# A triangular solve in two 8x8 blocks instead of one of 16x16, and an output norm whose channel scale and bias go into its other products

## The chip, the core and the metric

One core of a Trainium2 chip runs the kernel. Its engines are TensorE (PE, matrix products, with the loading of weights listed apart as PEld), VectorE (DVE), ScalarE (ACT), GpSimd (POOL) and SyncE (SP, which issues DMAs). Each has its own queue of instructions, worked off in order; they meet in SBUF and in PSUM, and wait for each other by semaphores. The metric is the device time of one execution in microseconds, the median of several runs.

## The reference, cut to what matters

One sequence of 256 tokens of width 1024 goes through two layers. Each layer is a feed-forward block, a mixer with three branches (a recurrent one with 8 heads of 64, a global attention and a window attention, each gated), and a second feed-forward block. The change is in the recurrent branch:

```python
def step(state, inp):                       # one token, one head; forwards and backwards over the sequence
    r_t, w_t, k_t, v_t, a_t, b_t = inp
    sa = jnp.einsum('bhij,bhj->bhi', state, a_t)
    state = (state * w_t[:, :, None, :] + sa[..., None] * b_t[:, :, None, :]
             + v_t[..., None] * k_t[:, :, None, :])
    return state, jnp.einsum('bhij,bhj->bhi', state, r_t)
...
mean = jnp.mean(wkv, axis=-1, keepdims=True)
var = jnp.mean(jnp.square(wkv - mean), axis=-1, keepdims=True)
y = ((wkv - mean) * lax.rsqrt(var + LNX_EPS)).reshape(bsz, s, RWKV_DIM) * lnx_g + lnx_b
y = y + bonus.reshape(bsz, s, RWKV_DIM)
gate = jax.nn.sigmoid(gl) @ g2
return y * gate
```

The sum over tokens is worked out in chunks of 64 tokens; within a chunk it needs the inverse of a unit lower triangular 64x64 matrix for each head and direction. Everything is float32.

## The kernel before, in words

Each matrix product of weights with activations is split: weights and activations are each a high part (`w_hi`, made by ACT or DVE at L62 or L64) and a rest (`w_lo`, made by DVE or GpSimd at L93), and three products are summed in PSUM (L52 is the line of every matmul, L55 that of every transpose on PE). Weights stream from HBM all the time. The feed-forward blocks are untouched by the change.

`Mixer.run` makes the mixer's work out of Python generators, one for each kind of work: Q (projections of the attentions), R (projections of the recurrent branch), A and V (attention scores and values), K (the normalised keys, `kk_norm`), P (`prep`, decay and learning rates), O (`post`, the output norm), F (`branches`: the gates `gt` and the output projections `wo`), and 0 to 3, the four units of the recurrence. Unit u has the head half `hf` = u//2 and the direction `d` = u%2. The string `ORDER` names, letter by letter, which generator goes on to its next `yield`. The strings in `ENG` name, for each kind of helper, the engine of each call in turn: a is ACT, v DVE, p GpSimd. A list scheduler of the framework then orders the instructions of each engine from this program, so the order of the rows on an engine isn't that of the letters alone.

In unit `wkv(u)`, `Lp` are products of 64x64 blocks, masked into `LL`; `T` are transposes, copied to `LL` and `Z`. When d is 1, the 16x16 diagonal blocks of both directions are copied into `sol` (`blocks()`, picks `K`), transposed so that each of them lies in one lane (L839), and solved by substitution on DVE (L842 to L851): for s from 1 to 14 a multiply (L847) and an add (L848). The result goes back by transposes (L852, L857: `Tn`). This happens once for each half: the first solve (unit 1) and the second solve (unit 3) of a layer, four in the program. From 16x16 to 32x32 one step of refinement on PE follows, `gp` (32 small matmuls a unit), a subtraction on DVE (L864) and `tp` (32 more), then L871 and the transposes L872; then the same from 32 to 64. The first `gp` and `tp` are worked off for both units d = 0 and 1 together.

`post()` takes the two halves in turn: the mean by a product with `bones`, the variance by `head_rsqrt` (products `hs`, DVE at L693, a power on GpSimd at L694, ACT at L696, products `hb` with the head's identity, which spread 1/rms over PSUM), then L985 (y times 1/rms), L988 (channel scale and bias), `bonp` (the bonus sum) and `gatep`, L995 (bonus times v), L996 (add) and L997 (times the gate). All of it is on DVE.

Of the kernel before, what the change touches and what calls it, by code (L numbers as in the profile page):

```python
# [11 lines left out]
ALU = mybir.AluOpType  # L12
AX = mybir.AxisListType
# [322 lines left out]
ORDER = 'QQQQQQRRQQRQKRRRQQARARAQARAKARRRKPVVAAARFARARVVPPAAAAAVFPVAAAAFFFVFVFFPFF00FF1F10F01011F1F010F01100F00001P12010F0F211111PF2OFFFPF23F233F3FO3F3223O2232F2332323323223F323OOOFFFFF'  # L336
ENG = {'Q': 'pvvxxxvwvvvv', 'R': 'xxwvxxvwvvvvvvv', 'F': 'wpxxxvppvpppxxpppwpvvwxxwpvvppppwxxp', 'M': 'vvvppvvv', 'O': 'vvvvvvvv', 'T': 'vavaaavvaaavavaa', 'G': 'vvavav', 'K': 'avaaaaavavaaaaaa', 'C': 'aavaavavvaavaavaaaaavaav', 'U': 'aavvavvaaaavavav', 'Y': 'avavvaavaaaaaavvavvaaaav', 'H': 'vvvv', 'J': 'vaavvaaa'}
KAP = float(np.exp(-0.5))
R_MU, R_W0, R_A0, R_KK, R_KA, R_RK, R_LG, R_LB, R_N = 0, 15, 23, 31, 35, 39, 43, 47, 51
# [16 lines left out]
class Mixer:  # L356
# [426 lines left out]
    def wkv(self, u):  # L783
        nc, n = self.nc, self.n
        V, mm = nc.vector, n.mm
        hf, d = u // 2, u % 2
# [3 lines left out]
        x = (v if d == 0 else v[:, :, ::-1]).rearrange("p a (c t) -> p a c t", c=4)  # L790
# [5 lines left out]
        if d == 1:  # L796
            scr = self.scr = self.t([128, 1024], "sol", tag="bk", bufs=2)
# [39 lines left out]
        if d == 1:  # L837
# [3 lines left out]
            Dm = Df.rearrange("p (t s) -> p t s", t=16)  # L841
            V.scalar_tensor_tensor(Dm, sol[:, :, 0:16], n.lane[:, 0:1], sol[:, :, 16:32], ALU.mult, ALU.add)  # L842
            stmp = scr[:, 768:832]
            for s in range(1, 15):
                m = 15 - s
                tv = stmp[:, :m * s].rearrange("p (t c) -> p t c", t=m)
                V.tensor_tensor(tv, Dm[:, s + 1:16, s:s + 1].to_broadcast([128, m, s]), Dm[:, s:s + 1, 0:s].to_broadcast([128, m, s]), ALU.mult)  # L847
                V.tensor_tensor(Dm[:, s + 1:16, 0:s], Dm[:, s + 1:16, 0:s], tv, ALU.add)  # L848
            V.memset(Df[:, 0:256:17], 1.0)
            V.tensor_scalar(sol[:, :, 0:16], Dm, n.lane[:, 0:1], None, ALU.mult)  # L850
# [3 lines left out]
        scr = self.scr  # L854
# [108 lines left out]
    def post(self):  # L963
        nc, n = self.nc, self.n
        V, mm = nc.vector, n.mm
        for hf in range(2):
# [18 lines left out]
            V.tensor_tensor(y, y, rb, ALU.mult)  # L985
            for pp in range(2):
                p = 2 * hf + pp
                self.pick("O").tensor_scalar(y[:, pp, :], y[:, pp, :], self.par[:, R_LG + p:R_LG + p + 1], self.par[:, R_LB + p:R_LB + p + 1], ALU.mult, ALU.add)  # L988
# [7 lines left out]
            self.pick("O").tensor_tensor(y, y, bon, ALU.add)  # L996
# [134 lines left out]
```

## Time and profile before

| | us |
|---|---|
| median of three runs | 1452.02 (1450.62 to 1454.06) |
| the profiled execution | 1456.31 |
| its span (first to last instruction) | 1454.4 |
| PE busy in the span | 1401.1 |
| DVE, ACT, POOL busy | 1004.6, 744.4, 206.2 |

The profile is of one execution, 4.3 us above the median. The span is 1.9 us shorter than that execution's time; the rest lies before the first and behind the last instruction. A row of the time line tells when instructions of one line started, how long they took, and in brackets how long the engine had been idle before and what it waited for. [...] "issue" is idle time for which the profile shows no cause.

### The profile page before, as it was taken

To read this page: it belongs to the slowest core of one execution; us is meant where nothing else is said; L and a number is where in the kernel's file an instruction comes from. 1 tells how busy PE (TensorE), PEld (TensorE's weight loads), DVE (VectorE), ACT (ScalarE), POOL (GpSimd) and SP (SyncE) were. 2 spreads that over 40 slices of the span, in tenths; PEclk is the share of its full clock that TensorE was granted. 3 is DMA by queue.
4 is the path that set the end of the run, shared out by engine and by line. 5 is a ranking of instruction groups with operands and counts; after the bars stand their busy time and mean duration, and the time that the engine had idled before them with its cause. 6 is when DMAs were issued, how large, how long until landed. Compare 5 with 4: busy or idle time off the path is not lost.

```text
span 1454.4 us, 25957 instructions
## 1 busy us (share of the span) xinstructions
PE 1401.1 (96%) x10482; PEld 1158.6 (80%) x10482; DVE 1004.6 (69%) x1518; ACT 744.4 (51%) x1241; POOL 206.2 (14%) x181
## 2 busy tenths in 40 slices
PE   7999999999998999999999999999998989999997
PEld 6888878877786878888888888788676868788886
DVE  5677467886867576776467864789758766668753
ACT  6555334665444355555455553356553443655543
POOL 0000033104315100000000000522041241000001
PEclk9999999999999999999999999999999999999999
DMA  7766656423314047666566666563243131576663
GB/s 219 209 201 187 195 152 190 130 70 120 113 50 144 27 144 205 189 191 194 162 188 196 190 192 191 159 182 100 67 132 102 49 114 48 167 207 188 189 191 112
DMA packets 113436, 220.24 MB, mean 151 GB/s; under 512 B 7362, under 2 KB 32164, under 8 KB 113316
## 3 DMA queue, kind: packets, MB, share of 16 engines
q1 hardware_dynamic: 111328, 215.08, 49.4%
q10 hardware_dynamic: 1508, 2.58, 0.5%
q8 instruction: 82, 1.34, 0.4%
q0 software_dynamic: 480, 0.93, 0.3%
q14 instruction: 38, 0.31, 0.1%
HBM read 217.51 MB, written 1.05 MB: 150 GB/s over the span
## 4 chain that ended last, share of the span: by engine, by line
PE 74%; DVE 8%; issue 8%; ACT 4%; DMA 3%; POOL 3%; SPq 0%; POOLq 0%; ACTq 0%; DVEq 0%
PE dn L52 19%; PE gt L52 18%; PE up L52 17%; PE gu L52 3%; PE wo L52 3%; PE rk L52 3%; DVE w_lo L93 2%; DMA w_raw<-in_w_in 2%; PE yp L52 1%; POOL w_lo L93 1%; PE Lp L52 1%; PE tp L55 1%; PE sc L52 1%; ACT w_hi L62 1%; DMA w_raw<-in_ffn_w_up 1%
## 5 line engine op out<-in xcount | busy, mean ns | idle before, releaser
L93 DVE TENSOR_TENSOR w_lo<-w_raw,w_hi 128x1024 fp32r<-128x1024 f32 (+1 forms) x360 | 444.1, 1234 | 252.0 <-ACT w_hi L62 248.5
L62 ACT ACTIVATE w_hi<-w_raw 128x1024 fp32r<-128x1024 f32 x358 | 379.8, 1062 | 403.4 <-PE dn L52 118.6
L52 PE MATMUL dn<-w_hi,aT 128*128 128x512 f32 x704 | 218.2, 390 | 0.0
L52 PE MATMUL gt<-hT,w_hi 128*128 128x512 f32 x512 | 179.0, 395 | 0.0
L52 PE MATMUL up<-hT,w_hi 128*128 128x512 f32 x512 | 178.2, 394 | 0.0
L52 PEld LDWEIGHTS dn<-w_hi,aT 128*128 128x128 f32 x704 | 131.9, 188 | 27.9 <-DVE sg L268 0.9
L93 POOL TENSOR_TENSOR w_lo<-w_raw,w_hi 128x1024 fp32r<-128x1024 f32 x50 | 123.5, 2474 | 149.4 <-ACT w_hi L62 91.1
L52 PE MATMUL gt<-hT,w_lo 128*128 128x256 f32 x512 | 142.2, 278 | 0.0
L52 PE MATMUL up<-hT,w_lo 128*128 128x256 f32 x512 | 141.8, 277 | 0.0
L52 PE MATMUL gt<-w_hi,hT 128*128 128x512 f32 x384 | 138.3, 421 | 0.0
L52 PE MATMUL dn<-w_lo,aT 128*128 128x512 f32 x352 | 137.7, 391 | 0.0
L52 PEld LDWEIGHTS up<-hT,w_hi 128*128 128x128 f32 x512 | 96.0, 188 | 22.3
L52 PEld LDWEIGHTS gt<-hT,w_hi 128*128 128x128 f32 x512 | 96.0, 188 | 22.1
L52 PEld LDWEIGHTS gt<-hT,w_lo 128*128 128x128 f32 x512 | 96.1, 188 | 0.2
L52 PEld LDWEIGHTS up<-hT,w_lo 128*128 128x128 f32 x512 | 96.1, 188 | 0.0
L52 PE MATMUL rk<-hT,w_hi 128*128 128x256 f32 x480 | 89.8, 288 | 4.0 <-DVE RKV L675 4.0
L52 PEld LDWEIGHTS gt<-w_hi,hT 128*128 128x128 f32 x384 | 73.0, 194 | 20.6 <-issue 5.2
L52 PEld LDWEIGHTS rk<-hT,w_hi 128*128 128x128 f32 x480 | 76.5, 194 | 6.9 <-DVE RKV L675 5.9
L52 PE MATMUL up<-w_hi,hT 128*128 128x512 f32 x256 | 81.4, 397 | 0.0
L52 PE MATMUL gt<-w_lo,hT 128*128 128x512 f32 x192 | 79.0, 411 | 0.0
L52 PEld LDWEIGHTS dn<-w_lo,aT 128*128 128x128 f32 x352 | 66.1, 188 | 14.8 <-DVE w_lo L93 1.4
L143 POOL TENSOR_SCALAR stat<-stat 128x1 f32<-128x1 f32 x14 | 3.4, 240 | 495.1 <-ACT gh L139 478.7
(272 smaller groups left out, 2427.9 us busy)
## 6 DMA issues: line engine op xcount, KB each, us to landing
w_raw<-in_ffn_w_up SPq DMA_DIRECT2D x160, 512.0 KB
w_raw<-in_w_in SPq DMA_DIRECT2D x102, 512.0 KB
w_raw<-in_ffn_w_down SPq DMA_DIRECT2D x88, 512.0 KB
w_raw<-in_ffn_w_up SPq DMA_DIRECT2D x32, 256.0 KB
w_raw<-in_w_out SPq DMA_DIRECT2D x16, 512.0 KB
w_raw<-in_w_o_ga SPq DMA_DIRECT2D x8, 512.0 KB
w_raw<-in_w_o_wa SPq DMA_DIRECT2D x8, 512.0 KB
w_raw<-in_w_o_rwkv SPq DMA_DIRECT2D x8, 512.0 KB
```

The costliest lines, as they stand in the source:

```text
L52: return self.nc.tensor.matmul(*a, **k)
L55: return self.nc.tensor.transpose(*a, **k)
L62: self.nc.scalar.activation(out, in_, AF.Copy, scale=1.0 if scale is None else scale)
L93: self.engine(on[1]).tensor_tensor(o, r, h.bitcast(F32), ALU.subtract)
L143: nc.gpsimd.tensor_scalar(self.ss[:, c:c + 1], self.ss[:, c:c + 1], 1.0 / D, EPS, ALU.mult, ALU.add)
```

## The change

There are four edits.

1. The solve. The two 8x8 diagonal blocks of each 16x16 matrix are inverted together, with one index more in each instruction: 6 steps of a multiply and an add (12 to 24 elements) instead of 14 (14 to 56). The block below the diagonal then is the inverse of the lower block, times the block, times the inverse of the upper: two rounds of a multiply over 512 elements (8x8x8, inputs broadcast, the right factor read transposed) and a reduction of 512 to 64.
2. The output norm. The multiply by 1/rms takes the channel scale with it, and the add of the bonus sum takes the bias: four instructions of 256 elements instead of two of 512 and two of 256.
3. `ORDER`. From `RRRKPVV` to `RRRPKVV`, from `VFFPFF00FF1F1` to `VFF0FF0PFF1F1`, and in the tail, where 0 to 3, P, F and O are put another way.
4. `ENG`. Of the picks `K` the eighth letter goes from v to a and the ninth from a to v: at the first solve ACT makes seven of the eight copies into `sol` and DVE one, where it was six and two; at the second, DVE makes two, where it was one.

The lines behind the solve have numbers 6 higher in the new file (L857 becomes L863, L864 L870, L871 L877, L872 L878); the solve's own are L849 and L850 (steps), L854 and L855 (product and reduction), L856 to L858.

```diff
-ORDER = 'QQQQQQRRQQRQKRRRQQARARAQARAKARRRKPVVAAARFARARVVPPAAAAAVFPVAAAAFFFVFVFFPFF00FF1F10F01011F1F010F01100F00001P12010F0F211111PF2OFFFPF23F233F3FO3F3223O2232F2332323323223F323OOOFFFFF'
+ORDER = 'QQQQQQRRQQRQKRRRQQARARAQARAKARRRPKVVAAARFARARVVPPAAAAAVFPVAAAAFFFVFVFF0FF0PFF1F10F01011F1F010F011000001001P120F01F21111PFF2OPFFFF23F233F3FO3F32223O2332F232323322323F323OOOFFFFF'
...
-ENG = {'Q': 'pvvxxxvwvvvv', 'R': 'xxwvxxvwvvvvvvv', 'F': 'wpxxxvppvpppxxpppwpvvwxxwpvvppppwxxp', 'M': 'vvvppvvv', 'O': 'vvvvvvvv', 'T': 'vavaaavvaaavavaa', 'G': 'vvavav', 'K': 'avaaaaavavaaaaaa', 'C': 'aavaavavvaavaavaaaaavaav', 'U': 'aavvavvaaaavavav', 'Y': 'avavvaavaaaaaavvavvaaaav', 'H': 'vvvv', 'J': 'vaavvaaa'}
+ENG = {'Q': 'pvvxxxvwvvvv', 'R': 'xxwvxxvwvvvvvvv', 'F': 'wpxxxvppvpppxxpppwpvvwxxwpvvppppwxxp', 'M': 'vvvppvvv', 'O': 'vvvvvvvv', 'T': 'vavaaavvaaavavaa', 'G': 'vvavav', 'K': 'avaaaaaavvaaaaaa', 'C': 'aavaavavvaavaavaaaaavaav', 'U': 'aavvavvaaaavavav', 'Y': 'avavvaavaaaaaavvavvaaaav', 'H': 'vvvv', 'J': 'vaavvaaa'}
...
-            stmp = scr[:, 768:832]
-            for s in range(1, 15):
-                m = 15 - s
-                tv = stmp[:, :m * s].rearrange("p (t c) -> p t c", t=m)
-                V.tensor_tensor(tv, Dm[:, s + 1:16, s:s + 1].to_broadcast([128, m, s]), Dm[:, s:s + 1, 0:s].to_broadcast([128, m, s]), ALU.mult)
-                V.tensor_tensor(Dm[:, s + 1:16, 0:s], Dm[:, s + 1:16, 0:s], tv, ALU.add)
+            D8 = scr[:, 512:784].rearrange("p (j x) -> p j x", j=2)[:, :, 0:128].rearrange("p j (t s) -> p j t s", t=8)
+            stmp = scr[:, 832:896]
+            for s in range(1, 7):
+                m = 7 - s
+                tv = stmp[:, :2 * m * s].rearrange("p (j t c) -> p j t c", j=2, t=m)
+                V.tensor_tensor(tv, D8[:, :, s + 1:8, s:s + 1].to_broadcast([128, 2, m, s]), D8[:, :, s:s + 1, 0:s].to_broadcast([128, 2, m, s]), ALU.mult)
+                V.tensor_tensor(D8[:, :, s + 1:8, 0:s], D8[:, :, s + 1:8, 0:s], tv, ALU.add)
             V.memset(Df[:, 0:256:17], 1.0)
+            low, prod, mid = Dm[:, 8:16, 0:8], scr[:, 0:512].rearrange("p (t c s) -> p t c s", t=8, c=8), scr[:, 832:896].rearrange("p (t c) -> p t c", t=8)
+            for left, right, to in ((low, Dm[:, 0:8, 0:8], mid), (Dm[:, 8:16, 8:16], mid, low)):
+                V.tensor_tensor(prod, left.unsqueeze(2).to_broadcast([128, 8, 8, 8]), right.rearrange("p s c -> p c s").unsqueeze(1).to_broadcast([128, 8, 8, 8]), ALU.mult)
+                V.tensor_reduce(to, prod, AX.X, ALU.add)
...
-            V.tensor_tensor(y, y, rb, ALU.mult)
             for pp in range(2):
                 p = 2 * hf + pp
-                self.pick("O").tensor_scalar(y[:, pp, :], y[:, pp, :], self.par[:, R_LG + p:R_LG + p + 1], self.par[:, R_LB + p:R_LB + p + 1], ALU.mult, ALU.add)
+                V.scalar_tensor_tensor(y[:, pp, :], y[:, pp, :], self.par[:, R_LG + p:R_LG + p + 1], rb[:, pp, :], ALU.mult, ALU.mult)
...
-            self.pick("O").tensor_tensor(y, y, bon, ALU.add)
+            for pp in range(2):
+                p = 2 * hf + pp
+                V.scalar_tensor_tensor(y[:, pp, :], y[:, pp, :], self.par[:, R_LB + p:R_LB + p + 1], bon[:, pp, :], ALU.add, ALU.add)
```

What this does to the order of instructions is shown at three places of layer 0. The first is PE behind the second solve: `gp` and `tp` are the small products of the refinement (x64 stands for both units of a half), `gt` the gate projections, `hb` and `bonp` the first post. Before:

```order
L52 MATMUL gt_4532<-w_hi,hT 128x512
L52 MATMUL gp<-Tn,LL 32x32 x64
L52 MATMUL gt_4533<-w_hi,hT 128x512
L52 MATMUL gt_4533<-w_lo,hT 128x512
L52 MATMUL gt_4533<-w_hi,hT 128x512
L52 MATMUL tp_4624<-sol,Tn 32x32 x32
L52 MATMUL tp_4663<-sol,Tn 32x32 x32
L52 MATMUL gt_4532<-w_hi,hT 128x512
L52 MATMUL gt_4532<-w_lo,hT 128x512
L55 MATMUL hb<-head,pz 128x128 x4
L52 MATMUL bonp<-pz,consts 128x256 x2
```

After:

```order
L52 MATMUL gp<-Tn,LL 32x32 x64
L52 MATMUL gt_4508<-w_hi,hT 128x512
L52 MATMUL gt_4508<-w_lo,hT 128x512
L52 MATMUL gt_4508<-w_hi,hT 128x512
L52 MATMUL tp_4600<-sol,Tn 32x32 x32
L52 MATMUL gt_4509<-w_hi,hT 128x512
L52 MATMUL gt_4509<-w_lo,hT 128x512
L52 MATMUL gt_4509<-w_hi,hT 128x512
L52 MATMUL gt_4508<-w_hi,hT 128x512
L52 MATMUL gt_4508<-w_lo,hT 128x512
L52 MATMUL gp<-Tn,LL 32x32 x16
L52 MATMUL tp_4658<-sol,Tn 32x32 x32
```

The two halves of `tp`, which followed each other, now have five `gt` and the next level's `gp` of one unit between them; behind them one `gt` is left ahead of `hb`. Ahead of `gp`, from the last transposes of unit 3 on, there are 18 `gt` instead of 21.

The second is PE at the post of the second half: `hs` starts the chain to 1/rms over DVE, GpSimd and ACT, and `hb` waits for its end; `wo` is the output projection of another branch. Before:

```order
L52 MATMUL hs<-consts,pz 128x2 x4
L52 MATMUL wo_5129<-w_hi,yT_4719 128x512
L52 MATMUL wo_5129<-w_lo,yT_4719 128x512
L52 MATMUL wo_5129<-w_hi,yT_4720 128x512
L52 MATMUL wo_5130<-w_hi,yT_4719 128x512
L52 MATMUL wo_5130<-w_lo,yT_4719 128x512
L52 MATMUL wo_5130<-w_hi,yT_4720 128x512
L52 MATMUL wo_5130<-w_hi,yT_4719 128x512
L52 MATMUL wo_5130<-w_lo,yT_4719 128x512
L55 MATMUL hb<-head,pz 128x128 x4
```

After:

```order
L52 MATMUL hs<-consts,pz 128x2 x4
L52 MATMUL wo_5105<-w_hi,yT_4714 128x512
L52 MATMUL wo_5105<-w_lo,yT_4714 128x512
L52 MATMUL wo_5105<-w_hi,yT_4715 128x512
L52 MATMUL wo_5105<-w_hi,yT_4714 128x512
L52 MATMUL wo_5105<-w_lo,yT_4714 128x512
L52 MATMUL wo_5105<-w_hi,yT_4715 128x512
L55 MATMUL hb<-head,pz 128x128 x4
L52 MATMUL bonp<-pz,consts 128x256
```

Six `wo` stand between `hs` and `hb` instead of eight.

The third is DVE at the end of the second solve: L64 makes the high part of a weight tile, L93 the rest, and L693 is the step of the first post that GpSimd waits for. Before:

```order
L850 TENSOR_SCALAR sol<-sol,consts 128x16x16
L851 TENSOR_SCALAR sol<-sol,consts 128x16x16
L64 CAST w_hi<-w_raw 128x1024
L852 STREAM_TRANSPOSE sol<-sol 128x16x2x16
L857 STREAM_TRANSPOSE Tn<-sol 128x256 x2
L864 TENSOR_TENSOR Tn<-gp,Tn 128x256 x2
L64 CAST w_hi<-w_raw 128x1024
L93 TENSOR_TENSOR w_lo<-w_raw,w_hi 128x1024
```

After:

```order
L854 TENSOR_TENSOR sol<-sol 128x512
L855 TENSOR_REDUCE sol<-sol 128x64
L693 TENSOR_SCALAR hss<-hs 128x8
L854 TENSOR_TENSOR sol<-sol 128x512
L855 TENSOR_REDUCE sol<-sol 128x8x8
L856 TENSOR_SCALAR sol<-sol,consts 128x16x16
L857 TENSOR_SCALAR sol<-sol,consts 128x16x16
L858 STREAM_TRANSPOSE sol<-sol 128x16x2x16
L64 CAST w_hi<-w_raw 128x1024
L863 STREAM_TRANSPOSE Tn<-sol 128x256 x2
L870 TENSOR_TENSOR Tn<-gp,Tn 128x256 x2
L877 SCALAR_TENSOR_TENSOR sol<-sol,tp_4600 128x256
```

The weight tile's high part, which stood ahead of the large transpose (L852 before), now stands behind it (L858). L693 stood between two of the small adds, and now stands behind the first reduction.

The orders on GpSimd and SP are the same as before.

## Rows read from the trace of the kernel before

**Rows 1.** The head of the page: the span, and each engine's busy time, its share of the span and its instructions.

```profile
span 1454.4 us, 25957 instructions
...
PE 1401.1 (96%) x10482; PEld 1158.6 (80%) x10482; DVE 1004.6 (69%) x1518; ACT 744.4 (51%) x1241; POOL 206.2 (14%) x181
```

**Rows 2.** The list of PE's waits, ordered by length: who waited <- for whom, us in total, times, longest. The first four rows are of the stretch 195 to 520 us (the mixer of layer 0), the last two of 910 to 1240 us (layer 1).

```profile
PE gp L52 <- DVE Tn L857: 5.2, 2, 4.0
PE tp L52 <- issue: 2.5, 2, 1.8
PE T L55 <- DVE LL L64: 1.3, 1, 1.3
PE ptp L55 <- DVE kkh L724: 0.7, 1, 0.7
...
PE gp L52 <- DVE Tn L857: 7.8, 2, 4.9
PE tp L52 <- issue: 1.7, 2, 1.5
```

**Rows 3.** DVE's time line at the second solve of layer 1: start in us, duration, engine, line, operation, out<-in, partitions x elements, count.

```profile
1175.48 0.18 DVE L847 TENSOR_TENSOR sol<-sol 128x14 f32<-128x14 f32 x1
...
1179.43 0.16 DVE L693 TENSOR_SCALAR hss<-hs 128x8 f32<-128x8 f32 x1
...
1182.09 0.35 DVE L850 TENSOR_SCALAR sol<-sol,consts 128x256 f32<-128x256 f32 x1
...
1182.62 0.69 DVE L64 CAST w_hi<-w_raw 128x1024 fp32r<-128x1024 f32 x1
1183.22 1.05 DVE L852 STREAM_TRANSPOSE sol<-sol 128x512 f32<-128x512 f32 x1
1184.30 0.77 DVE L857 STREAM_TRANSPOSE Tn<-sol 128x256 f32<-128x256 f32 x2
```

**Rows 4.** PE's time line at the first and the second solve of layer 1, with the same columns; in brackets the idle time before the row and what ended it.

```profile
1114.09 0.72 PE L52 MATMUL tp<-sol,Tn 32*32 32x32 f32 x61 [0.20 <-issue]
...
1117.76 0.24 PE L52 MATMUL gp<-Tn,LL 32*32 32x32 f32 x2 [0.48 <-issue]
...
1178.73 0.39 PE L52 MATMUL gt<-w_lo,hT 128*128 128x512 f32 x1
1178.96 0.62 PE L52 MATMUL gt<-w_hi,hT 128*128 128x512 f32 x2
...
1184.89 1.93 PE L52 MATMUL gp<-Tn,LL 32*32 32x32 f32 x128 [4.87 <-DVE Tn L857]
...
1188.33 1.03 PE L52 MATMUL tp<-sol,Tn 32*32 32x32 f32 x97
1190.90 0.45 PE L52 MATMUL tp<-sol,Tn 32*32 32x32 f32 x31 [1.54 <-issue]
```

**Rows 5.** PE's time line at the last post of layer 0 (505 us) and at the first post of layer 1 (1191 us), and one row of the view by windows: window, its length, busy us of PE, PEld, DVE, ACT and POOL with their instructions, then the granted clock, the DMA share and GB/s.

```profile
505.06 0.66 PE L55 MATMUL hb<-head,pz 128*128 128x128 f32 x4 [0.67 <-ACT pz L696]
505.55 0.60 PE L52 MATMUL bonp<-pz,consts 128*128 128x256 f32 x2
505.98 0.59 PE L52 MATMUL gatep<-LG,lora 128*128 128x256 f32 x2
...
1191.90 1.05 PE L55 MATMUL hb<-head,pz 128*128 128x128 f32 x4
...
1194.10 1.32 PE L52 MATMUL gt<-w_hi,hT 128*128 128x512 f32 x2
1195.26 1.03 PE L52 MATMUL gatep<-LG,lora 128*128 128x256 f32 x4
...
1193.00:1194.00 1.00, 1.00 (x3) 0.76 (x3) 0.68 (x1) 0.98 (x3) 0.00 (x0) 0.50 0.41 156
```

**Rows 6.** The instructions of lines L676, L560 and L839 over the whole run (min/median/max ns), and two L848 at the second solve of layer 1 from the view by lines in the windows 1175.65 to 1175.75 and 1181.85 to 1181.95 us (busy us, mean ns): the first is step 1 of the solve, the second step 14.

```profile
L676 DVE TENSOR_TENSOR RKV<-RKV,projpad x12: 679/691/693, 245.3 to 1022.0; 128x512 f32<-128x512 f32 x12
...
L560 DVE TENSOR_REDUCE at<-sc x32: 679/684/694, 260.6 to 1051.6; 128x2 f32<-128x512 f32 x32
...
L839 DVE STREAM_TRANSPOSE sol<-sol x4: 1064/1086/1117, 371.8 to 1171.0; 128x512 f32<-128x512 f32 x4
...
L848 DVE TENSOR_TENSOR sol<-sol 128x14 f32<-128x14 f32 x1 | 0.2, 182 | 0.0
...
L848 DVE TENSOR_TENSOR sol<-sol 128x14 f32<-128x14 f32 x1 | 0.2, 174 | 0.0
```

**Rows 7.** Time lines of layer 0: ACT at the copies for the first solve, DVE in the first solve, and DVE at the normalised keys.

```profile
369.21 2.55 ACT L62 ACTIVATE sol<-LL 32x256 f32<-32x256 f32 x6
...
385.76 1.22 DVE L93 TENSOR_TENSOR w_lo<-w_raw,w_hi 128x1024 fp32r<-128x1024 f32 x1
...
282.62 0.82 DVE L515 TENSOR_TENSOR att<-at 128x640 f32<-128x640 f32 x1
```

**Rows 8.** Time lines of DVE and GpSimd (POOL) behind the first solve of layer 0, and of GpSimd at the second solve of layer 1.

```profile
396.89 1.13 DVE L64 CAST w_hi<-w_raw 128x1024 fp32r<-128x1024 f32 x1 [0.27 <-PE gt L52]
...
395.10 2.38 POOL L93 TENSOR_TENSOR w_lo<-w_raw,w_hi 128x1024 fp32r<-128x1024 f32 x1 [11.28 <-DVE w_hi L64]
...
1183.00 4.83 POOL L93 TENSOR_TENSOR w_lo<-w_raw,w_hi 128x1024 fp32r<-128x1024 f32 x2 [1.69 <-ACT w_hi L62]
```

**Rows 9.** The instructions of L988 over the whole run (min/median/max ns).

```profile
L988 DVE TENSOR_SCALAR yacc<-yacc,par x8: 403/406/415, 475.1 to 1227.1; 128x256 f32<-128x256 f32 x8
```

## The prediction

> **What bounds the kernel now.** I read the page first: TensorE (PE) is busy 96% of the span [rows 1], so the kernel is as long as its matmuls plus the time in which PE stands still or runs at its lower clock. The change adds and removes no matmul. The second view is therefore the list of PE's waits in the two stretches that hold the mixers, 195–520 and 910–1240 us [rows 2]. The reader should see there that the longest waits are all at one place in the code: `gp`, the first product behind the triangular solve, waits for DVE's transposes `Tn` at L857, 5.2 us in layer 0 and 7.8 us in layer 1, and behind it `tp` stops for "issue", 2.5 and 1.7 us. Everything else that the change touches is a wait of 0.7 to 1.3 us: `T` and `ptp` there, `hb` at 505.06 in [rows 5]. What the change can win is thus about 17 us at the most, 1.2%.
>
> The third view is DVE's time line at the second solve of layer 1 [rows 3]. The 28 small multiplies and adds run from 1175.48 to 1182.09, 6.61 us, and nothing else is on DVE but a memset and L693: DVE is the bound there. PE runs out of `gt` and gets `gp` at 1184.89 after 4.87 us [rows 4]. So a microsecond taken from the solve is a microsecond of PE there. The fourth view, PE's time line [rows 4], shows the second loss: `tp` breaks off after 97 of its 128 matmuls and goes on at 1190.90 after 1.54 us of "issue": nothing the profile knows of holds it. I read it as the supply of instructions. The two stops at the first solve of layer 1, 1114.09 and 1117.76, are 128 matmuls apart (61 of `tp`, five `gt`, 62 of `gp`), and the small matmuls go by at 0.011 us each, where a `gt` takes 0.23 (1178.73 to 1178.96). [...]
>
> [...]
>
> [...] `hb`, four `bonp` and two `gt` take 3.36 us there (1191.90 to 1195.26). At the full clock `hb` takes 0.49 and two `bonp` 0.43 (505.06, 505.55, 505.98), so 1.35 for the first five, and two `gt` 0.46: 1.81. The slow stretch costs 1.5 us.
>
> **The change part by part, for one layer.** *The solve's work.* The 28 small operations go, 0.236 each by 6.61/28 [rows 3], memset and L693 included. There come 12 of them, 2.83; two reductions of 512 elements, 0.684 each by L560 [rows 6], with 0.03 to the next, 1.43; and two products of 512 elements whose one input is read 64 or 32 bytes apart. The trace has no such product. From below it is L676, 0.69 for 512 elements of two contiguous inputs; from above L839, a transpose of 512 that walks by strides, 1.09 [rows 6]. The nearest rows are two L848 of 14 elements: 0.182 us at step 1, where inputs and output lie 64 bytes apart, and 0.174 at step 14, where they lie side by side: 8 ns for 14 elements in three streams, some 0.2 to 0.3 ns for each element of one stream. 512 elements at 0.3 ns are 0.15; I take 0.84, with 0.03 to the next 0.87. The solve is 2.83 + 1.43 + 1.74 = 6.00, a gain of 0.61 (0.91 by the lower bound, 0.11 by the upper).
>
> [...]
>
> *Second solve.* DVE's CAST of weights (0.60 up to the next instruction, 1182.62) moves from ahead of the large transpose to between it and `Tn`; it stays in the chain, and only the overlap of two independent instructions, 0.1, is gained. `gp` comes 0.71 earlier. But 18 `gt` instead of 21 now stand ahead of it, so PE has 3 × 0.23 = 0.69 less to do meanwhile: PE's idle time there changes by −0.02. The three `gt` come back behind `gp`: five `gt` stand between the two halves of `tp`, where before the 64 ran in one piece. They are 5 × 0.23 = 1.15 us of work ahead of the point at which the supply ran out (it is fixed by the count of instructions and lies about at the start of the second half), so the stop of 1.54 becomes 0.4: −1.15. With so short a stop I expect no second fall of the clock: −1.5. The wait before `gp` stays near 5 us, so the slow stretch behind `gp` stays too.
>
> *First solve.* On DVE the same 0.61 goes, a second L93 (1.22 at 385.76 [rows 7], less 0.1 of overlap) comes ahead of the last transposes, and of two 512-element operations on `gth` and `merged`, 0.6 each by L676 less the overlap, one is left ahead of them instead of two: −0.61 + 1.12 − 0.60 = −0.09. One more `gt` ahead of `gp` hides 0.23; the two `gt` that stood between `gp` and `tp` are gone, and they covered the subtraction that `tp` waits for and delayed the stop behind it: +0.46. Sum +0.14.
>
> *The letter in the K picks.* ACT copies seven blocks of the first solve instead of six, DVE one instead of two. Six took 2.55 [rows 7], so the transpose L839, and the `LL` copy behind it that PE waits for at `T`, come 0.43 later: +0.43. DVE had finished its two sooner, so its lighter load gives nothing back. For the second solve the copies end long before their use: 0.
>
> *The order strings.* `kkh` (L724) now comes behind L515, 0.82 us [rows 7], and `lw` and `la` ahead of the last `hb`; `ptp` waits for `kkh`. Of 0.82 the moved small matmuls cover about 0.5: +0.3 (0 to 0.8). At the second post `hb` waits for a chain from `hs` over DVE, GpSimd and ACT; six 0.23 us matmuls stand between `hs` and `hb` instead of eight, and the chain doesn't change: +0.46 on the 0.67 it waits now. Orders of SP and GpSimd are unchanged, so no DMA is issued behind another one.
>
> *The output norm.* One 512-element multiply, two 256-element operations (0.406 by L988 [rows 9]) and one 512-element add become four 256-element operations. On DVE that is some 0.5 us less in each post. At the first post the next PE work waits for none of it, at the second other weights' work fills PE: 0. One operation now reads two SBUF inputs and can be held up by GpSimd as in [rows 8]: 0 to +0.5.
>
> **The sum.** −0.02 − 1.15 − 1.5 + 0.14 + 0.43 + 0.3 + 0.46 = −1.34 for a layer, −2.7 us for two. The profiled execution took 1456.3 us, 4.3 above the median of the runs; the terms are differences, so I set them against the median: 1452.0 − 2.7 = **1449.3 us**. A measurement of this kernel can tell about 0.2% (2.9 us) from no change, so this is at the edge. Its own range, with the products between their bounds (−1.2 to +2.0 us over the four solves) and `ptp` between 0 and 0.8, is 1447 to 1452.
>
> **Rivals.** *1. The stop stays.* If the instructions' arrival is set by something that moves with the work (the weight loads that start behind `gp`, say), the five `gt` only move the idle time and the clock falls again: −1.15 and −1.5 drop out, leaving +1.31 a layer: 1454.6 us. For it: no row names what the supply waits for. Against it: the count of 128 matmuls between two stops.
>
> *2. Slower: the CAST is caught behind GpSimd.* A CAST at 396.89 took 1.13 instead of 0.69; it ended 0.54 after GpSimd's `w_lo` of 395.10 did [rows 8]. At the second solve GpSimd runs two `w_lo` in a row from 1183.00, 4.83 us, and before the change DVE's CAST started 0.38 ahead of them, at 1182.62. After it L693, which starts the chain to GpSimd, stands behind the first reduction: 1175.48 + 2.83 + 0.87 + 0.71 = 1179.89 instead of 1179.43, so GpSimd starts at 1183.46; the CAST starts at 1175.48 + 6.00 + 0.53 + 0.98 = 1182.99, 0.47 ahead. Each product adds its excess twice to the CAST and once to GpSimd, so it decides from 1.31 us for a product. Then `gp` comes 2.4 later (one of the two `w_lo`), and four solves are 8 × 0.47 = 3.8 longer: 1449.3 + 3.8 + 4.8 = 1458 us.
>
> *3. The products cost no more than contiguous ones.* 8 × 0.15 = 1.2 less, and with the waits at `ptp` and `hb` covered (−1.5): 1446.6 us.
>
> *4. It doesn't shorten the solve.* Products of 1.15 each make the solve as long as it was, short of what rival 2 needs: 1449.3 + 4 × 0.61 = 1451.7 us.
>
> **How the numbers follow.** Forecast 0.50 (0.28 faster, 0.22 within 0.2%), rival 1 0.18 (0.11 within, 0.07 slower), rival 2 0.10 (slower), rival 3 0.10 (faster), rival 4 0.12 (0.10 within, 0.02 faster). That is faster 0.40, same 0.43, slower 0.17. The range runs from below rival 3 to rival 1's time and leaves out rival 2: 1445.5 to 1455.
>
> **What would show it.** Right: DVE from the first small multiply to the last transpose's start 0.5 to 0.7 shorter; products near 0.84; `tp`'s stop under 0.7 in both second solves, and the clock at full by `hb`; `T` waiting 1.7 and the second `hb` 1.1. Wrong: a CAST over 1 us between the two transposes of a second solve, a stop of 1.5 us again, a clock of 0.50 under `bonp`, or a new stop of over 1 us at a first solve, where `tp` now follows `gp` directly.

## The result and the profile after

The changed kernel took 1461.22 us (median of 19 runs, from 1454.67 up), the kernel before, on the same chips, 1452.30 (19 runs, 1443.64 to 1461.29). The ratio is 1.0067, with a 95% interval from 1.0049 to 1.0084: slower by about 9 us. The forecast was 1449.3, its range ended at 1455. Four single runs of 1715 to 7710 us (one each of the changed kernel, e7, e8 and e15) count in the medians of the time, but in no ratio, clock loss or rest below.

The profiled execution of the changed kernel took 1467.48 us, 6.3 above its median. The head of its page:

```profile
span 1465.6 us, 25895 instructions
...
PE 1407.8 (96%) x10482; PEld 1162.1 (79%) x10482; DVE 1011.4 (69%) x1470; ACT 744.9 (51%) x1241; POOL 207.8 (14%) x181
```

Against [rows 1] the matmuls are the same 10482; PE is busy 6.7 us longer and idle 4.5 us longer (1465.6 − 1407.8 = 57.8 instead of 53.3). The same matmuls took longer, so the first thing to look for is the clock. The idle time is in the list of PE's waits (us in total, times, longest). First the stretch 195 to 530 (layer 0), then 910 to 1260 (layer 1), last one row of the kernel before in layer 1:

```profile
PE gp L52 <- DVE Tn L863: 7.1, 2, 4.0
...
PE yp L52 <- DVE at L64: 2.0, 2, 1.4
PE T L55 <- DVE LL L64: 1.5, 1, 1.5
...
PE dn L52 <- ACT hT L128: 1.2, 1, 1.2
PE tp L52 <- issue: 1.2, 1, 1.2
PE hb L55 <- ACT pz L696: 1.1, 1, 1.1
...
PE gp L52 <- DVE Tn L863: 4.0, 1, 4.0
...
PE yp L52 <- DVE at L64: 1.9, 2, 1.3
PE tp L52 <- issue: 1.7, 1, 1.7
```

```profile
PE yp L52 <- DVE at L64: 1.4, 1, 1.4
```

Beside [rows 2], `gp` has 7.1 + 4.0 = 11.1 us instead of 13.0, "issue" 2.9 instead of 4.2, and `ptp`'s wait of 0.7 a layer for `kkh` is gone. `T` and `hb` are longer, `dn` at the end of the mixer waits 1.2 us in each layer, which it didn't, and `yp`, the product of attention scores and values, waits 3.9 us for DVE's copies `at` instead of 1.4. `gp`, "issue" and `ptp` gain less than the others lose: the sum is more waiting, not less.

**The second solve** went as forecast. PE's time line there in layer 1:

```profile
1195.83 1.68 PE L52 MATMUL gp<-Tn,LL 32*32 32x32 f32 x128 [4.05 <-DVE Tn L863]
...
1199.01 1.03 PE L52 MATMUL tp<-sol,Tn 32*32 32x32 f32 x64
1199.98 0.50 PE L52 MATMUL gt<-w_hi,hT 128*128 128x512 f32 x1
...
1203.10 0.66 PE L55 MATMUL hb<-head,pz 128*128 128x128 f32 x4
```

No row between `gp` and `hb` carries an idle time, where [rows 4] have 1.54 us of "issue" (in layer 0 the stop of 1.8 us of [rows 2] is gone too), and `hb` and `bonp` run at a granted clock of 1.00 (a share of the full TensorE clock), where [rows 5] show 0.50. The first and the last row are 7.27 us apart, before 7.01 (1184.89 to 1191.90), with four more `gt` and the next level's first `gp` and `tp` between them. The clock not granted from the pause to the products behind `hb` is 1.7 us in layer 1, before 3.4; in layer 0 it is 3.4 in both profiles.

**The first solve** went wrong. PE's time line there in layer 0, the kernel before and then the changed one:

```profile
391.12 1.35 PE L52 MATMUL gp<-Tn,LL 32*32 32x32 f32 x128 [1.20 <-DVE Tn L857]
392.40 0.50 PE L52 MATMUL gt<-w_hi,hT 128*128 128x512 f32 x1
392.74 0.40 PE L52 MATMUL gt<-w_lo,hT 128*128 128x512 f32 x1
393.49 0.94 PE L52 MATMUL tp<-sol,Tn 32*32 32x32 f32 x86 [0.35 <-DVE Tn L864]
395.11 0.57 PE L52 MATMUL tp<-sol,Tn 32*32 32x32 f32 x42 [0.69 <-issue]
```

```profile
395.27 1.93 PE L52 MATMUL gp<-Tn,LL 32*32 32x32 f32 x128 [3.01 <-DVE Tn L863]
397.11 1.47 PE L52 MATMUL tp<-sol,Tn 32*32 32x32 f32 x87
399.81 0.79 PE L52 MATMUL tp<-sol,Tn 32*32 32x32 f32 x41 [1.23 <-issue]
```

The same 128 `gp` take 1.93 us instead of 1.35: they ran at a granted clock of 0.50, before at 1.00. `tp` stands directly behind them and stops for 1.23 us. The view by windows of the changed kernel (window, length, busy us of PE, PEld, DVE, ACT, POOL, granted clock, DMA share, GB/s):

```profile
394.00:395.00 1.00, 0.00 (x0) 0.00 (x0) 1.00 (x3) 0.00 (x0) 0.00 (x0) 0.66 0.71 72
395.00:396.00 1.00, 0.72 (x54) 0.73 (x58) 1.00 (x3) 0.00 (x0) 0.00 (x0) 0.50 0.71 258
...
405.00:406.00 1.00, 1.00 (x3) 0.64 (x3) 0.94 (x3) 0.00 (x0) 0.00 (x0) 0.50 0.00 0
...
414.00:415.00 1.00, 1.00 (x5) 0.35 (x4) 0.24 (x1) 0.00 (x0) 0.00 (x0) 0.60 0.06 16
415.00:416.00 1.00, 1.00 (x6) 0.51 (x4) 0.00 (x0) 0.00 (x0) 0.00 (x0) 1.00 0.00 0
```

PE stands idle from 392.3 on, the granted clock falls in 394, and it is back at 1.00 only in 415. All windows between those shown have 0.50. The clock not granted is 0.34 + 19 × 0.50 + 0.40 = 10.2 us, with PE busy in most of it. Nothing like it is in the two mixers of the profile of before, whose stretches of low clock each add up to 3.4 us at the most. It has more of them, though: over the whole span the two profiles lose 22.0 and 17.5 us (span × (1 − mean clock)).

**The two products** of the solve, all eight of the run (min/median/max ns), and their reductions:

```profile
L854 DVE TENSOR_TENSOR sol<-sol x8: 1047/1084/2978, 386.9 to 1191.3; 128x512 f32<-128x512 f32 x8
...
L855 DVE TENSOR_REDUCE sol<-sol x8: 676/686/686, 388.0 to 1192.4; 128x64 f32<-128x512 f32 x8
```

The products are at the upper bound of the forecast, L839's 1.09 us [rows 6], not at 0.84. The longest, 2978, started at 1112.83, half a microsecond behind a `w_lo` of GpSimd.

### The profile page after: what moved, and what is told of

Read it like the earlier page. It is cut to its first block, busy times and chain, and to the rows that moved or that the text cites. A ratio compares the mean times of both kernels' runs of the same rounds, so it can differ in the third digit from the quotient of the medians.

```text
span 1465.6 us, 25895 instructions
## 1 busy us (share of the span) xinstructions
PE 1407.8 (96%) x10482; PEld 1162.1 (79%) x10482; DVE 1011.4 (69%) x1470; ACT 744.9 (51%) x1241; POOL 207.8 (14%) x181
## 3 DMA queue, kind: packets, MB, share of 16 engines
q8 instruction: 82, 1.34, 0.4%
## 4 chain that ended last, share of the span: by engine, by line
PE 71%; DVE 11%; issue 8%; ACT 4%; DMA 3%; POOL 3%; SPq 0%; POOLq 0%; ACTq 0%; DVEq 0%
PE dn L52 19%; PE up L52 17%; PE gt L52 16%; PE gu L52 3%; PE rk L52 3%; PE pj L52 2%; DVE w_lo L93 2%; PE wo L52 2%; POOL w_lo L93 1%; DMA w_raw<-in_w_in 1%; PE yp L52 1%; PE tp L55 1%; DMA w_raw<-in_ffn_w_up 1%; ACT w_hi L62 1%; ACT at L568 1%
## 5 line engine op out<-in xcount | busy, mean ns | idle before, releaser
L93 DVE TENSOR_TENSOR w_lo<-w_raw,w_hi 128x1024 fp32r<-128x1024 f32 (+1 forms) x360 | 442.2, 1229 | 258.7 <-ACT w_hi L62 257.2
L93 POOL TENSOR_TENSOR w_lo<-w_raw,w_hi 128x1024 fp32r<-128x1024 f32 x50 | 128.0, 2565 | 167.8 <-ACT w_hi L62 90.7
```

Of the source, the lines that this page charges most:

```text
L93: self.engine(on[1]).tensor_tensor(o, r, h.bitcast(F32), ALU.subtract)
```

## The experiments

Each run lists the span and the mean granted clock. **Clock loss** is span × (1 − mean clock), **rest** is the span less that; medians over the runs of each kernel. The mean clock is given to three digits, so the clock loss of a run comes in steps of 1.5 us. The kernel before, run beside each group of experiments, had a clock loss of 14.5 to 15.9 and a rest of 1432.7 to 1437.0.

| run | what it is | us | ratio to before, 95% interval | clock loss | rest |
|---|---|---|---|---|---|
| after | the change (19 runs) | 1461.22 | 1.0067, 1.0049 to 1.0084 | 22.7 | 1437.4 |
| e5_after_again | the change once more | 1463.91 | 1.0076, 1.0053 to 1.0100 | 22.7 | 1438.5 |
| e1_solve | the solve alone | 1458.09 | 1.0035, 1.0023 to 1.0047 | 16.7 | 1439.1 |
| e2_order | `ORDER` alone | 1461.55 | 1.0062, 1.0049 to 1.0075 | 19.7 | 1440.5 |
| e6_kpick | the K letters alone | 1468.18 | 1.0112, 1.0087 to 1.0138 | 25.6 | 1441.3 |
| e8_post | the output norm alone | 1460.09 | 1.0044, 1.0022 to 1.0065 | 16.0 | 1440.5 |
| e3_noorder | all but `ORDER` | 1455.88 | 1.0014, 0.9996 to 1.0032 | 17.5 | 1435.9 |
| e4_nosolve | all but the solve | 1468.17 | 1.0111, 1.0088 to 1.0133 | 16.1 | 1447.5 |
| e7_nok | all but the K letters | 1468.95 | 1.0111, 1.0082 to 1.0140 | 22.0 | 1442.7 |
| e9_gts_between | the change, four `gt` between `gp` and `tp` | 1454.17 | 1.0027, 1.0013 to 1.0041 | 14.5 | 1437.9 |
| e10_gts_ahead | the change, 23 `gt` ahead of `gp` | 1468.75 | 1.0127, 1.0106 to 1.0149 | 23.5 | 1444.2 |
| e11_product_order | the change, strided read moved to the reduction | 1458.35 | 1.0066, 1.0043 to 1.0088 | 20.4 | 1436.1 |
| e12_between_tail | e9, and `dn` no longer waits | 1453.94 | 1.0011, 0.9997 to 1.0024 | 14.5 | 1437.1 |
| e13_oldorder_between | e3, `gt` between | 1452.88 | 1.0006, 0.9995 to 1.0017 | 13.1 | 1437.7 |
| e14_before_between | before, `gt` between | 1452.40 | 1.0010, 0.9994 to 1.0026 | 13.0 | 1437.4 |
| e15_old_between_tail | e13, and `dn` no longer waits | 1450.41 | 0.9988, 0.9971 to 1.0004 | 11.6 | 1436.2 |
| e16_old_between_tail_b | the same, another pair of letters | 1449.34 | 0.9983, 0.9964 to 1.0002 | 11.6 | 1435.4 |

**The parts alone: e1_solve, e2_order, e6_kpick, e8_post.** Each has one of the four edits of the diff above and nothing else; the smallest of them reads

```diff
-'K': 'avaaaaavavaaaaaa'
+'K': 'avaaaaaavvaaaaaa'
```

> Only the solve is changed (two 8x8 blocks), order strings, picks and output norm as before. Theory A (the order strings, with the longer PE pauses ahead of T and of the first gp, bring on low-clock stretches; the solve is innocent): 1449 to 1453 us, no slower than before, gp's wait at the second solves 0.3 to 0.5 us shorter, two products near 1.07 us each. Theory B (the solve itself is the loss, its products cost 1.05 to 1.1 and meet GpSimd at the first solve): 1457 to 1462 us, first gp waiting 2.5 us or more in a layer.

> Only ORDER is changed; solve, picks and output norm as before. Theory A: 1457 to 1463 us, with low-clock stretches of 10 us or more lost in the mixers beyond those of before. Theory B: within 2 us of before, since the old solve stays.

> Only the letter of the K picks is changed. It moves two gt from between gp and tp to behind tp at the first solve, puts eight more ahead of gp, and T waits 0.15 to 0.45 us longer. Theory C: slower by 3 to 7 us, nearly all of it lost clock behind T and behind the first gp. Rival (the picks are harmless, the ORDER does it): within 2 us of before.

> Only the output norm is changed. The first solve's order on PE stays that of before. Both theories: within 2 us of before, 0.5 us less of DVE in each post; a wait at the end of the mixer (dn for ACT's hT, 1.2 us) would be from this edit if it shows here.

e1_solve lies in the range of theory B, e2_order in that of theory A, though with 5.2 us more clock loss than before and not 10; e6_kpick (+16 us) and e8_post (+6) lie above both of theirs. All four are slower, and their sum (0.35 + 0.62 + 1.12 + 0.44 = 2.5%) is nearly four times what the whole change costs: the parts don't add up. The dearest is the smallest edit, a copy of some 0.4 us moved from DVE to ACT and one moved back. What it does on PE isn't near that copy at all. The list scheduler puts 14 `gt` ahead of the first `gp` instead of six and none between `gp` and `tp`. PE's time line there in layer 0 of e6_kpick:

```profile
391.16 1.35 PE L52 MATMUL gp<-Tn,LL 32*32 32x32 f32 x128 [1.12 <-DVE Tn L857]
393.00 0.75 PE L52 MATMUL tp<-sol,Tn 32*32 32x32 f32 x64 [0.48 <-DVE Tn L864]
...
396.02 1.08 PE L52 MATMUL tp<-sol,Tn 32*32 32x32 f32 x64 [2.27 <-DVE Tn L864]
```

The subtraction that `tp` needs, covered in part by two `gt` before, is now waited for, and the second half of `tp` is slower (1.08 against 0.75 for 64). Of e6's loss against the kernel before, run beside it, 10.4 us are clock and 5.8 rest. With the output norm alone `hb` waits 1.7 us, with `ORDER` alone 1.6 and `wo` another 1.7.

**The parts taken away: e3_noorder, e4_nosolve, e7_nok**, each the whole change without one edit, and e5_after_again, the changed kernel itself on another chip.

> The whole change but with the ORDER of before (new solve, output norm and picks). Theory A: 1449 to 1454 us. Theory B: 1457 to 1463 us.

> The whole change but with the solve of before (new ORDER, output norm and picks). Theory A: 1458 to 1464 us, as slow as the whole change or slower. Theory B: 1450 to 1454 us.

> The whole change with the K picks of before. T waits 1.3 us again, but no gt stands ahead of the first gp, whose pause becomes 4 us or more. Theory C: about as slow as the whole change (1459 to 1464 us), with the low clock behind the first gp instead of behind T. Rival (the picks' T wait is the trigger): 1452 to 1456 us.

> The changed kernel once more, for a second profile and for the split of its time into the span less what the low clock takes (span x (1 - mean granted clock)) and the rest. Theory C (what the change loses is granted clock, brought on by the pauses at T and at the first gp, and not standstill): rest equal to that of before within 2 us, some 7 us more lost to the clock, the lost stretches at T or at the first gp. Rival (standstill and longer work): rest 6 to 9 us above before, clock loss equal.

Without the new `ORDER` the change is 0.14% above before, with an interval from −0.04% to 0.32% (its time lies between the two ranges that were expected), so most of the loss needs that string. Without the solve or the K letters it is slower still, and slower than either theory put it, so neither is the cause by itself. That is not all clock: against the kernel before, run beside them, e4 has 1.6 us more clock loss and 10.5 more rest, e7 6.8 and 7.2. In e4's profile `Lp` and `wo` each wait 3.6 us for two layers at places where the changed kernel doesn't wait. The K letter's own size can be read off here: `T` waits 1.5 us in e3, e4, e5 and e6, which have it, and 1.3 in before, e1, e2, e7 and e8, which don't.

e5_after_again has the same instructions, and its profiled execution took 1455.03 us, near the fastest of the kernel. Its time line of PE at the first solve of layer 0, and a window there:

```profile
393.76 1.35 PE L52 MATMUL gp<-Tn,LL 32*32 32x32 f32 x128 [0.25 <-DVE Tn L863]
395.59 0.75 PE L52 MATMUL tp<-sol,Tn 32*32 32x32 f32 x64 [0.48 <-DVE Tn L870]
396.52 0.38 PE L52 MATMUL tp<-sol,Tn 32*32 32x32 f32 x23 [0.18 <-DVE Tn L870]
398.16 0.56 PE L52 MATMUL tp<-sol,Tn 32*32 32x32 f32 x41 [1.26 <-issue]
...
398.00:399.00 1.00, 0.84 (x43) 0.75 (x44) 0.23 (x1) 0.98 (x3) 1.00 (x1) 1.00 0.00 0
```

The stop of 1.26 us is here too, at the same matmul, but `gp` waited 0.25 instead of 3.01, and the clock stays at 1.00. So here the stop costs its 1.26 us and no clock. The pause is short because the clock fell earlier, behind `T`, where both executions wait 1.48 us:

```profile
380.00:381.00 1.00, 1.00 (x4) 0.81 (x3) 0.97 (x5) 0.00 (x0) 0.00 (x0) 0.50 0.51 78
```

The clock is below 1.00 from 376 to 384 (3.4 us lost) in e5 and at 1.00 there in the other profile. The `gt` behind `T` then take longer (four matmuls in 380 to 381, in the other profile six) and fill the time until `Tn` is there. `gp` starts 17.9 us behind that `T` in e5 and 17.7 in the other, so the clock lost there costs next to nothing.

The changed kernel's runs scatter with the clock: over the 18 that are compared the clock loss lies between 13.1 and 32.3 us, and goes with the time (correlation 0.90; 0.96 over the 12 runs of e5).

**What stands between `gp` and `tp`: e9_gts_between.** The theory by now: with no `gt` between them, `tp` runs into the stop while the clock is low. The rival: the pause ahead of `gp` is what counts. The edit exchanges two letters of the new `ORDER` (the 89th and the 91st), so that four `gt` stand between `gp` and `tp` and the same seven ahead:

```diff
-...F0PFF1F10F01011F1F010F011000001001P...
+...F0PFF1F10F01011F0F110F011000001001P...
```

> The whole change with two letters of ORDER exchanged (the 1 and the 0 around the F at the first solve), which puts four gt between gp and tp there and leaves the second solve and the work ahead of the first gp as they are. Theory C (low clock kept up by the stop of tp that follows gp directly): the 'issue' stop at the first solve under 0.5 us, clock loss down from 22.7 to some 17 us, time 1454 to 1458 us; rest of the time unchanged at 1437 to 1439. Rival (the clock loss is brought on by the pause ahead of gp or at T, the stop has no part): clock loss 21 to 24 us, 1460 to 1464 us.

The ratio is 1.0027 instead of 1.0067, 5.8 us less, and what the medians show of it is clock: a loss of 14.5 instead of 22.7, the rest 1437.9 and 1437.4. Of e9's remaining 0.27% none is clock: the kernel before, run beside it, had a loss of 15.9 and a rest of 1432.7. PE's time line at the same place, and the windows:

```profile
390.12 1.93 PE L52 MATMUL gp<-Tn,LL 32*32 32x32 f32 x128 [3.02 <-DVE Tn L863]
391.99 0.80 PE L52 MATMUL gt<-w_lo,hT 128*128 128x512 f32 x1
392.58 1.05 PE L52 MATMUL gt<-w_hi,hT 128*128 128x512 f32 x2
393.43 0.63 PE L52 MATMUL gt<-w_lo,hT 128*128 128x512 f32 x1
393.99 1.93 PE L52 MATMUL tp<-sol,Tn 32*32 32x32 f32 x128
...
389.00:390.00 1.00, 0.00 (x0) 0.00 (x0) 1.00 (x4) 0.00 (x0) 0.00 (x0) 0.76 0.36 111
...
395.00:396.00 1.00, 1.00 (x72) 0.94 (x61) 0.83 (x3) 0.41 (x1) 0.91 (x1) 0.50 0.06 16
396.00:397.00 1.00, 1.00 (x4) 0.85 (x5) 0.75 (x3) 0.96 (x4) 0.00 (x0) 0.82 0.09 8
```

The pause ahead of `gp` is the same, 3.02 us, and the clock falls in it as before; but nothing stops behind it, and the clock is back in 396, after 0.24 + 6 × 0.50 + 0.18 = 3.4 us instead of 10.2. In 12 runs the loss never exceeds 18.9.

**The rival: e10_gts_ahead.** Two other letters are exchanged so that 23 `gt` cover the pause ahead of `gp`:

```diff
-...F0PFF1F10F01011F1F010F01...
+...F0PFF1F1F001011F1F010F01...
```

> The whole change with two other letters exchanged (0 and F), which puts 23 gt instead of 7 ahead of the first gp and two inside tp; T's wait and the second solve stay. If the pause ahead of the first gp is the trigger: that pause under 0.5 us, clock loss 14 to 17 us, time 1449 to 1455 us. If the pause at T or something elsewhere is: clock loss still above 20 us, 1458 us or more.

It is the slowest of all the variants of the change. The pause ahead of the first `gp` is 1.67 us instead of 3.01 in layer 0, but 3.22 in layer 1, and the `gt` are missing elsewhere: `T` waits 2.9 us instead of 1.5, `tp` 1.9 for its subtraction, and the clock loss stays at 23.5. In its profile that is ten stretches of 1.7 to 3.4 us, none as long as the changed kernel's. So much else moved that this run decides nothing on the pause; e9 does, which keeps the pause and is rid of the 10 us.

**The product's read: e11_product_order.** The multiply reads rows side by side, and the reduction walks by strides instead:

```diff
-    V.tensor_tensor(prod, left.unsqueeze(2)..., right.rearrange("p s c -> p c s").unsqueeze(1)..., ALU.mult)
-    V.tensor_reduce(to, prod, AX.X, ALU.add)
+    V.tensor_tensor(prod, left.unsqueeze(3)..., right.unsqueeze(1)..., ALU.mult)
+    V.tensor_reduce(to, prod.rearrange("p t s c -> p t c s"), AX.X, ALU.add)
```

> The whole change with the 512 products of a round laid out so that the multiply reads both factors along rows and writes in order, and the reduction reads by strides of 32 bytes instead. Same sums; order of instructions on all engines unchanged. If the strided read of one factor is what made a product 1.07 us: multiplies 0.69 to 0.75, and the reductions tell whether a strided read costs there too (0.69 or 1.0). If the broadcast in four dimensions is: multiplies stay at 1.05 to 1.1. In time: 0 to 3 us less than the change.

```profile
L854 DVE TENSOR_TENSOR sol<-sol x8: 691/693/1590, 385.0 to 1189.9; 128x512 f32<-128x512 f32 x8
...
L855 DVE TENSOR_REDUCE sol<-sol x8: 1066/1139/1210, 385.7 to 1190.6; 128x64 f32<-128x512 f32 x8
```

The product fell by 0.39 us (1084 to 693) and the reduction rose by 0.45 (686 to 1139). So the strided read of 512 elements costs 0.39 us in the product and 0.45 in the reduction, and the ratio stays as it was, 1.0066.

The profile of e11 also shows the long stretch without a pause or a low clock ahead of it. PE's time line at the first solve of layer 1, and a window behind it:

```profile
1113.98 1.35 PE L52 MATMUL gp<-Tn,LL 32*32 32x32 f32 x128 [0.48 <-DVE Tn L863]
...
1118.15 0.70 PE L52 MATMUL tp<-sol,Tn 32*32 32x32 f32 x58 [1.15 <-issue]
...
1119.00:1120.00 1.00, 1.00 (x5) 0.64 (x4) 0.76 (x2) 0.98 (x3) 0.79 (x1) 0.87 0.06 16
```

`gp` and the first part of `tp` run at a granted clock of 1.00. It falls only behind the stop, in 1119, and is back in 1137: 8.5 us.

**The rest: e12_between_tail to e16_old_between_tail_b.** e12 is e9 with two more letters exchanged in the tail, so that the twelve `tp` of `merged` stand together ahead of `dn`. e13 is e3, and e14 the kernel before, with the letters of e9 exchanged in the old string. e15 and e16 are e13 with a pair of letters in the tail exchanged, at two places:

```diff
# e12
-...F232323322323F323...
+...F232323232323F323...
# e13, e14
-...1011F1F010F01100F...
+...1011F0F110F01100F...
# e15
-...F2332323323223F323...
+...F2332323233223F323...
# e16
-...F2332323323223F323...
+...F233232332322F3323...
```

> The kernel with the four gt between gp and tp, and two more letters exchanged near the end (a 3 and a 2), which puts the first three transposes of merged side by side again ahead of dn, as before the change. If dn's wait for ACT's hT (1.2 us a layer) is the part of the rest that exceeds the kernel before: that wait gone, the rest 2 to 2.5 us less, time 1450 to 1453 us. If not: as with the four gt alone, ratio 1.002 to 1.004.

> New solve, output norm and picks with the ORDER of before, in which the same two letters are exchanged, so that four gt stand between gp and tp at the first solve; the second solve keeps its tp in one piece. Theory C: clock loss 13 to 15 us instead of 17.5 without the exchange, ratio to before 0.997 to 1.001. Rival (the low clock follows the pauses ahead of gp and at T, whatever follows them): as without the exchange, 1.0014.

> The kernel before with the same two letters exchanged: four gt instead of two between gp and tp at the first solve, nothing else of the change. Theory C: stops of tp at the first solve gone (0.69 and 0.20 us), clock loss equal or 1 us less, ratio 0.998 to 1.000. Rival: no difference beyond the interval, or slower for two gt less elsewhere (1.000 to 1.002).

> The new solve, the new output norm and the new K letter with the order of before, the two letters at the first solve exchanged as in the run called e13_oldorder_between, and in the tail two letters exchanged so that four out_proj products no longer stand ahead of dn. If the wait of dn is a cost of its own, it goes here as it did in e12_between_tail, and with it up to 1.2 us a layer: 2.4 us less than e13_oldorder_between's difference, so 0.998 to 0.9995 of before. If that wait was only time that another wait takes over, 1.0006 as in e13_oldorder_between. Clock lost 13 to 15 us in both cases.

> The same as e15_old_between_tail, with the pair of letters in the tail exchanged at another place. Both theories as there: 0.998 to 0.9995 if dn's wait is a cost of its own, 1.0006 if not; a difference of more than 0.15% between the two kernels would say that what else the scheduler moves weighs more than dn's wait.

In e12 `dn`'s wait is gone and `hb` waits 0.7 instead of 1.1: 0.0016 less than e9 by the two ratios, whose intervals overlap. In e13 the clock loss is 4.4 us below e3's, which has no `gt` there either, and in e14 1.5 below before's, where two stood there already; the rest takes back 1.8 and 1.9 of that. In time neither gain is clear of noise (1.0006 against e3's 1.0014, and 1.0010 for e14, which was expected at 0.998 to 1.000). The gain is smaller than in e9, since e3 had less clock loss to give back than the changed kernel (17.5 against 22.7). e15 and e16 lose no time at `dn` and have the least clock loss of all, 11.6. They are the only ones below the kernel before, by 1.2 and 1.7 thousandths, with intervals that just reach 1. Against the changed kernel they win 11 to 12 us; that one beats the kernel before isn't shown.

**The 18 profiled executions side by side** (the kernel before, the changed one and the 16 runs, two layers each) show how far the account holds. At the first solve of layer 0 the pause ahead of `gp` goes with the clock behind `T`: 2.7 to 3.5 us in the seven that lost none there, 0.8 to 1.7 in the six that lost 1.7 us, 0.25 to 0.41 in the five that lost 3.4. So the 3.01 us are not the change's: the kernel before has 1.20 in layer 0, with 1.7 us lost behind `T`, and 2.91 in layer 1, with none. Behind `gp`, the 18 first solves with two or four `gt` between `gp` and `tp` have no stretch of low clock that loses more than 3.4 us. Of the 18 with none, five lose 8.5 to 10.2: the changed kernel and e11 in layer 0, e4, e7 and e11 in layer 1. The other 13 have no stretch over 3.4, though pause, low clock and stop can all be there: in layer 0 of e1 and e7, behind a pause of 3.45 and 3.40 us, the clock comes back during the stop of 1.15 and 1.20 us, and 1.7 us are lost. So the missing `gt` make the long stretch possible, not certain.

## Why the prediction was wrong

**The step that failed** is "First solve ... Sum +0.14". It priced the two `gt` that stood between `gp` and `tp` at +0.46, "they covered the subtraction that `tp` waits for and delayed the stop behind it", at 0.23 us for a `gt`, its time at a granted clock of 1.00. That was the right place, and the last item of "What would show it" names it, but the prediction applied its own view of the clock only to the second solve. There it gave 1.5 us to a stop that brings a second fall. At the first solve it took away the work between pause and stop and priced no clock. By e9, whose edit is at that place, it cost 8.2 us of clock, 5.8 us by the ratios. In e5_after_again, against the kernel before that ran beside it, the whole difference is 7.5 us of clock (22.7 against 15.2) and 3.0 of rest (1438.5 against 1435.5).

**The products** (0.87 each with the gap, from 0.84) take 1.09 and 1.13 at the second solve of layer 1. DVE's time line there:

```profile
1184.81 2.25 DVE L849 TENSOR_TENSOR sol<-sol 128x12 f32<-128x12 f32 x1
...
1189.45 1.05 DVE L854 TENSOR_TENSOR sol<-sol 128x512 f32<-128x512 f32 x1
1190.54 0.69 DVE L855 TENSOR_REDUCE sol<-sol 128x64 f32<-128x512 f32 x1
...
1191.26 1.10 DVE L854 TENSOR_TENSOR sol<-sol 128x512 f32<-128x512 f32 x1
1192.39 0.69 DVE L855 TENSOR_REDUCE sol<-sol 128x64 f32<-128x512 f32 x1
1193.11 0.35 DVE L856 TENSOR_SCALAR sol<-sol,consts 128x256 f32<-128x256 f32 x1
...
1194.66 0.67 DVE L64 CAST w_hi<-w_raw 128x1024 fp32r<-128x1024 f32 x1
```

From 1184.81 to 1193.11 are 8.30 us, of which one step, caught beside a `w_lo` of GpSimd (1184.36, 2.67 us), has 2.07 too many: 6.23 instead of 6.61, a gain of 0.38, not 0.61. The bound from L839 was nearer than the pair of L848, whose 8 ns between 174 and 182 for 14 elements don't show what 512 cost. The price of the error is 4 × 0.23 = 0.9 us. Rival 4's premise came near, its time did not.

**The second solve** was right in mechanism: the stop gone, the clock back ahead of `hb`, the wait ahead of `gp` 4.05 in both layers (4.00 and 4.87 before). Its −1.5 of clock came in layer 1 (3.4 to 1.7 us), but not in layer 0, where the one stretch behind the pause is as long as the two were (3.4 us). The −1.5 is the 3.36 us of [rows 5], at the 0.50 shown there, less 1.81. The −1.15 was worked out from a supply of instructions, which no run shows; what they show is that the 1.54 us of "issue" are gone there. Rival 1 is out. **Rival 2** is out where it was placed: the CAST took 0.67. DVE was held up beside a `w_lo` of GpSimd elsewhere, though: the small step took 2.25 and ended 0.03 us behind that `w_lo`, a product took 2.98 (1112.83) and ended 1.09 behind its own (1112.32, 2.40 us). It is no new cost, since the kernel before also has a small step of 2.31 us at 381.59.

**The K letter** gave `T` 0.2 instead of 0.43 a layer. **`hb`** waits 1.1 as forecast, though not by the new string alone: e3 has the same without it, and e12 has 0.7 with two letters of the tail exchanged. **The order strings** were priced at `ptp` alone in that place, 0.3 longer, and its wait on `kkh` is gone, 0.7 shorter. What the sum left out is `yp`: it waits 2.0 and 1.9 us a layer for `at` instead of 0 and 1.4, and over both layers 3.5 to 4.3 us in all nine profiles with the new `ORDER` against 0 to 1.4 in the nine with the old one. **The output norm** was put at 0; alone it costs 0.44%, with `hb` waiting 1.7 us a layer and the `tp` of `merged` 1.0, and not on DVE but by the order that it brings. "The next PE work waits for none of it" looked only at the post. `dn` behind the mixer now waits 1.2 us a layer for the last `hT`; e2 has that wait with the new `ORDER` alone, e3 with the three other edits, and none of those alone (e1, e6, e8). It was in no term, 2.4 us for two layers; by e9 and e12, removing it and the 0.4 at `hb` is worth about 2, with intervals that overlap.

What stays open: why the kernels with one edit have a rest 2 to 6 us longer, and e4 and e7 one of 10.5 and 7.2, since their waits, like those at `yp`, were only read, not undone; why the clock falls behind `T` in one execution and not in another of the same program after the same wait; and why, with no `gt` behind `gp`, the clock is back after 3 to 4 us in some executions and after 17 to 20 in others.

## What to carry to other kernels

Where an engine pauses for another, look at what stands directly behind the pause. Here no stretch of low clock behind `gp` cost more than 3.4 us with two or four large matmuls between two runs of small ones, five of 18 cost 8.5 to 10.2 with none, and two letters of an order decided 6 to 8 us. Price every place where an edit removes filler between two such runs, with the clock and not only with the waits. And where a list scheduler sets the order, an edit is priced by the order it gives on the whole engine: four edits that cost 2.5% one by one cost 0.7% together.

## What the runs showed of the hardware

The stop for "issue" goes with the sequence of instructions: with no `gt` ahead of `tp` it stood at the same 41 last matmuls with the granted clock at 0.50 (after, 1.23 us) and at 1.00 (e5, 1.26 us). With four `gt` ahead of `tp` the clock matters too: there was no stop where `gp` ran at a granted clock of 0.50 (both layers of e9, layer 1 of e12, e14, e15 and e16), and one of 0.34 to 1.34 us where it ran at 1.00 (layer 0 of e12 to e16, layer 1 of e13). No run shows what PE waits for in these stops.

After a pause of 3.0 us the granted clock was 0.50 for 6.8 us with four `gt` behind `gp` (3.4 us lost; e9), and for 20.5 us with `tp` and the stop behind it (10.2 lost; after); after 3.4 us, with the same behind it, for 3.4 us (1.7 lost; e7, layer 0).

A clock lost ahead of a wait can cost nothing: 3.4 us lost behind `T` in e5 shortened the pause ahead of `gp` from 3.01 to 0.25 us.
